# A two-block hybrid network on one core: the first three products in plain fp32, running totals on VectorE, decay triangles by a product, and a port rule in the planner

## The chip, the cores and the metric

The kernel runs on one core of a Trainium2 chip. The metric is the device time in microseconds (us) of one execution, the median of several. The engines are TensorE (PE; PEld is its weight load), VectorE (DVE), ScalarE (ACT), GpSimd (POOL), and SyncE (SP), which here only issues DMAs. In fp32r a 32-bit operand takes one pass through TensorE; a plain fp32 operand takes a slower form, which the profile records as two matmul records for each product.

## The reference, cut to what matters

Two blocks of two layers each run over 272 tokens (16 meta tokens and 256 of the sequence, width 1024), later over 256. The first layer is a gated delta rule, and its start is what the change touches:

```
a_in = rms_norm(hs, norm_w[0, 0])
proj = a_in @ w_in                      # q, k, v, z, and 2 x 16 gate columns
g = -exp(a_log) * softplus(proj[gates] + dt_bias)
G = cumsum(g)                           # in chunks
decay = exp(where(i >= j, G_i - G_j, -inf))
a_mat = I + (k_i . k_j) beta_i * decay * strict ;  attn = (q_i . k_j) * decay
```

After it come an output product, an RMS norm, the residual, a convolutional FFN of width 2816, an mLSTM layer and a second such FFN. The second block has short convolution and windowed attention, a SwiGLU FFN, gated linear attention with latent attention, and another SwiGLU FFN; each of its four parts ends in a LayerNorm.

## The kernel before

Activations lie transposed: 128 features on the partitions, tokens along the free axis, eight tiles of 128 for width 1024. The weights stream from HBM in 413 chunks of 512 KB, and one chunk is eight tiles of 128x128, which is one output tile of a product over 1024 features. Every chunk (`wload`, from L309) is split in two fp32r halves: ACT copies the raw tile to `wh` (L325), DVE subtracts to get `wl` (L326). An activation is split likewise into `xh` and `xl`. A product is then three fp32r matmuls (`mm3`): wh with xh, wh with xl, wl with xh. There are three raw buffers, and a raw buffer is free once both halves are made.

**The opening** (`first_raw`, then `pre_norm` called from `gdn`). x times the norm's weight is split without waiting for the row statistic, and three products start from it: the 32 gate columns and two tiles of q and k. `group` interleaves them (L372 to L375); the results are multiplied by 1/rms afterwards (L525). In the same time DVE and ACT write the normed x and its split (L479, L473, L474), from which all further products run. From the gates come the decays: for each of four groups of heads DVE makes `gl` (three instructions, L712), PE sums it along the tokens with plain fp32 products (L716), ACT takes the exponential (called on L717, recorded as L270) and POOL multiplies by a triangle of ones (L718), twelve times in all.

**The norms.** `post_norm` runs the output product tile by tile; ACT squares, and POOL adds the squares into a running total `acc` (`acc_sq`, L444). After the last tile a column sum of `acc` and one of the last square go to one PSUM bank, DVE forms mean + eps (`rse` L552, `rsv` L553), POOL raises to the power -1/2 (L554), PE broadcasts (L429). Then, for each of the eight tiles, DVE multiplies (`xn` L561) and adds the residual (`hs` L563), ACT makes `xh` (L567), DVE `xl` (L568), ACT the next square (L571), and POOL adds it to the next running total; meanwhile PE runs the next layer's first products from `xh` and `xl` through `group`. Three of the four calls have this second total. `warm` puts dummy products on PE meanwhile (L414). `layer_norm` has its running totals on POOL too (L1251, L1259, L1265), eleven additions in each of four calls.

**The order of the work.** `IssueOrder` takes all instructions, gives each a modelled cost, and simulates the five engines forward and backward, three rounds; `fix` then ties each engine's instructions in the order found. That fixes the order within each engine. Between engines only data and buffers order the work, at run time. In its model VectorE and GpSimd share a port: an instruction in `port` waits while the other engine's one is running.

Of the kernel before, what the change touches and what calls it, by code (L numbers as in the profile page):

```python
# [6 lines left out]
F32 = mybir.dt.float32  # L7
F32R = mybir.dt.float32r
AF = mybir.ActivationFunctionType
ALU = mybir.AluOpType  # L10
# [248 lines left out]
class Kern:  # L259
# [49 lines left out]
    def wload(self, first, need, ahead):  # L309
# [3 lines left out]
        while self.wloaded <= need or (self.wloaded <= need + ahead and self.wloaded < self.io["w"].shape[0]):  # L313
# [13 lines left out]
            self.wchunks[self.wloaded] = (h, l)  # L327
            self.wloaded += 1

    def wnext(self, first=None):  # L330
        ci, j = divmod(self.wpos, CH)
        self.wpos += 1
        if j == 0:
            self.wload(ci if first is None else first, ci, self.ahead if first is None else 0)
        h, l = self.wchunks[ci]
        return h[:, j], l[:, j]
# [104 lines left out]
    def acc_sq(self, acc, prev, sq, m):  # L441

        if m and m < KD - 1:
            self.nc.gpsimd.tensor_tensor(acc, prev if m == 1 else acc, sq, ALU.add)  # L444

    def rsqrt(self, v, pool):
        V = self.nc.vector
# [34 lines left out]
    def first_raw(self, pool):  # L482

        nc, n = self.nc, T1
        raw = [pool.tile([128, 4, T1], F32R, name="xr", tag="of", bufs=4) for _ in range(4)]
        xh, xl = [lambda k, a=a: raw[a + k // 4][:, k % 4] for a in (0, 2)]
        sqs = [pool.tile([128, 2, 2, T1], F32, name="kq", bufs=4) for _ in range(2)]
        st = self.pst.tile([128, 512], F32, name="st")[:, :n]
        for k in range(KD):
            hs = self.hs[:, k]  # L490
            nc.scalar.activation(xh(k), hs, AF.Copy, scale=self.p("nw00", k))
            nc.vector.scalar_tensor_tensor(xl(k), hs, self.p("nw00", k), xh(k).bitcast(F32), ALU.mult, ALU.subtract)
            if k % 2:
                j = k // 2
                sq, hs = [a.rearrange("p a b t -> p (a b) t")[:, 2 * (j % 2):2 * (j % 2) + 2] for a in (sqs[j // 2],)][0], self.hs[:, k - 1:k + 1]
                if j % 2:
                    nc.vector.tensor_tensor(sq, hs, hs, ALU.mult)
                else:
                    nc.scalar.activation(sq, hs, AF.Square)
                if j:  # L500
                    nc.vector.tensor_tensor(acc, acc, sq, ALU.add)
                else:
                    acc = sq
        for i in range(2):
            self.stat_add(st, acc[:, i], i == 0, i == 1)
        return st, lambda k: (xh(k), xl(k))

    def pre_norm(self, wname, t0, pool, items, outs, dest=None, st=None, tag="rsy"):

        nc, n = self.nc, T1 - t0  # L510
        s = [] if st is None else [st]

        def hook():
            if not s:
                s.append(self.row_stat(*self.nacc, n))

        raw = self.group(items, hook)
        r = self.rstd(s[0], n, D, pool, tag)
        xh, xl = dest or [pool.tile([128, KD, n], F32R, name=a) for a in ("xnh", "xnl")]
        outs = list(outs(raw))  # L520
        for k in range(KD):
            self.scaled(k, xh, xl, wname, t0, n, r, pool)
            if k and outs:
                o, ps, p, t = outs.pop(0)
                nc.vector.tensor_tensor(o, ps, r[:p, t:], ALU.mult)  # L525
        assert not outs
        return lambda k: (xh[:, k, :n], xl[:, k, :n])

    def post_norm(self, wname, K, x, t0, pool, nxt, tag='mix'):

        nc, n = self.nc, T1 - t0
        V = nc.vector
        mixt = [pool.tile([128, 4, T1], F32, name="mix", tag=tag + (str(i + 1) if tag == "PT" else ""), bufs=1 if tag == "PT" else 2)
                for i in range(2)]
        mix = lambda m: mixt[m // 4][:, m % 4, :n]
        acc = self.small.tile([128, T1], F32, name="acc")[:, :n]
        prev = None
        first = self.halves(x, n) if K == 16 else []
        for m in range(KD):
            ps = first.pop(0) if first else self.proj(K, x, n)  # L540
            sq = pool.tile([128, T1], F32, name="sq", bufs=2)[:, :n]
            nc.scalar.activation(sq, ps, AF.Square)
            nc.scalar.activation(mix(m), ps, AF.Copy, scale=self.p(wname, m))
            self.acc_sq(acc, prev, sq, m)
            prev = sq
        self.lnexp()
        c = len(starts(n))
        st = self.bank()
        self.stat_cols(st, acc, n)
        self.warm(6, self.stat_cols(st[:, c:], sq, n))  # L550
        e, v = [self.small.tile([128, 4], F32, name=a)[:, :c] for a in ("rse", "rsv")]
        V.tensor_scalar(e, st[:, 0:c], 1.0 / D, 1e-6, ALU.mult, ALU.add)  # L552
        V.scalar_tensor_tensor(v, st[:, c:2 * c], 1.0 / D, e, ALU.mult, ALU.add)  # L553
        nc.gpsimd.tensor_tensor(v, v, self.c("nhalf")[:, :c], ALU.pow)  # L554
        r = self.pst.tile([128, 512], F32, name="st")[:, :n]
        self.warm(8, self.bcast(r, v, n))
        xh, xl = self.xsplit()
        acc = self.small.tile([128, T1], F32, name="acc")[:, :n]
        for m in range(KD):
            t = pool.tile([128, T1], F32, name="xn", bufs=2)[:, :n]  # L560
            V.tensor_tensor(t, mix(m), r, ALU.mult)  # L561
            hs = self.hs[:, m, t0:]
            V.tensor_tensor(hs, hs, t, ALU.add)  # L563
            if nxt is None:
                self.split(xh[:, m, :n], xl[:, m, :n], hs)
                continue
            nc.scalar.activation(xh[:, m, :n], hs, AF.Copy, scale=self.p(nxt, m))  # L567
            V.scalar_tensor_tensor(xl[:, m, :n], hs, self.p(nxt, m), xh[:, m, :n].bitcast(F32), ALU.mult, ALU.subtract)  # L568
            sq = (self.small.tile([128, T1], F32, name="sql", bufs=1) if m == KD - 1 else
                  pool.tile([128, T1], F32, name="sq", bufs=2))[:, :n]  # L570
            nc.scalar.activation(sq, hs, AF.Square)  # L571
            self.acc_sq(acc, prev, sq, m)
            prev = sq
        self.nacc = (acc, sq)
        return lambda k: (xh[:, k, :n], xl[:, k, :n])
# [41 lines left out]
    def gdn(self):  # L617
# [5 lines left out]
        with ExitStack() as es:  # L623
# [11 lines left out]
            for t in Ufs + X64s:  # L635
# [6 lines left out]
            ba = v_first[0:32, 2]  # L642
            wg = pool.tile([128, KD, 32], F32, name="wg", tag="o1")
            nc.scalar.dma_start(wg, self.io["wg"].rearrange("p (k m) -> p k m", m=32))
            wgs = pool.tile([128, 2, KD, 32], F32R, name="wgs", tag="vs1")
            wgh, wgl = wgs[:, 0], wgs[:, 1]
            self.split(wgh, wgl, wg)
            x = self.pre_norm("nw00", 0, pool, [(xr, T1, 32, True, [(wgh[:, k], wgl[:, k]) for k in range(KD)]), (xr, T1, 128, False), (xr, T1, 128, False)],
                              lambda ps: [(ba, ps[0], 32, 0), (v_first[:, 0], ps[1], 128, 0), (v_first[:, 1], ps[2], 128, 0)],
                              self.xsplit(), st, "cv")  # L650
            ba16 = pool.tile([32, 4, 32], F32, name="cv", bufs=2)
            G.memset(ba16, 0.0)
            V.tensor_copy(ba16[:, :, 0:16], ba[:, 0:16].unsqueeze(1).to_broadcast([32, 4, 16]))
# [49 lines left out]
            strict = pool.tile([128, 2, 128], F32, name="strict", tag="o0")  # L703
            V.tensor_tensor(strict[:, 0], self.ones, self.c("tri"), sub)
            V.tensor_tensor(strict[:, 1], self.c("blk16"), self.c("tri16"), sub)
            for g in range(4):
                eg_ = pool.tile([128, 9, 128], F32, name=f"E{g}")
                gl = pool.tile([128, 9, 128], F32, name="gl_", tag=("PT0", "PT1", "PT2", "vs0")[g])
                for c in range(3):
# [2 lines left out]
                    V.tensor_tensor(gl[:, u], strict[:, c // 2].unsqueeze(1).to_broadcast([128, nn, 128]),  # L712
                                    gg[:, 9 * g + 4 * c:9 * g + 4 * c + nn].unsqueeze(2).to_broadcast([128, nn, 128]), mult)
                    tp = bank().rearrange("p (h i) -> p h i", h=4)
                    for h in range(nn):
                        TE.matmul(tp[:, h], gl[:, 4 * c + h], self.c("tri" if c < 2 else "tri16"), start=True, stop=True)  # L716
                    self.act(eg_[:, u], tp[:, 0:nn], AF.Exp)  # L717
                    G.tensor_tensor(eg_[:, u], eg_[:, u], self.c("tri" if c < 2 else "tri16").unsqueeze(1).to_broadcast([128, nn, 128]), mult)  # L718
                E.append(eg_)

            self.silu()
# [496 lines left out]
    def layer_norm(self, name, K, x, pool, last=False, tags=("xr0", "xr1", "xr2", "xr3")):  # L1218
# [27 lines left out]
        def square(m):  # L1246
# [1 line left out]
            sq = tmp("lnsq", 3)  # L1248
            nc.scalar.activation(sq, X[:, m], AF.Square)
            if 1 <= m < KD - 1:  # L1250
                GP.tensor_tensor(ac2, prev if m == 1 else ac2, sq, add)  # L1251
            prev = sq

        for m in range(KD):
            ps = self.proj(K, x, n)
            if m < 4:
                V.scalar_tensor_tensor(X[:, m], X[:, m], ALPHA, ps, mult, add)
                if m:
                    GP.tensor_tensor(ac, X[:, 0] if m == 1 else ac, X[:, m], add)  # L1259
            else:  # L1260
                V.tensor_tensor(X[:, m], X[:, m], ps, add)
                square(m)
                not_normed(m)
                if 4 < m < KD - 1:
                    GP.tensor_tensor(ac, X[:, 4] if m == 5 else ac, X[:, m], add)  # L1265
            if m == 3:
                st = self.pst.tile([128, 512], F32, name="st")[:, :n]
                self.stat_add(st, ac, True, True)
# [432 lines left out]
class IssueOrder:  # L1701
# [207 lines left out]
    def forward(self, due, look=0):  # L1909
# [30 lines left out]
        while True:  # L1940
# [13 lines left out]
            if best > 100.0:  # L1954
                wait[e].remove(chosen)
                heapq.heapify(wait[e])
                push(now[e], chosen[1:])
            d, k = pop(now[e])
            t = max(t, ready[k])
            if self.port[k] and owner != e:  # L1960
                t = max(t, shared)
# [110 lines left out]
```

## Time and profile before

| what | value |
|---|---|
| median of 3 runs | 1469.59 us (1467.21 to 1471.34) |
| the profiled execution | 1478.24 us, of which 1476.40 us from first to last instruction |
| PE, DVE, ACT, POOL busy | 98%, 71%, 57%, 13% |
| mean granted clock of TensorE | 0.988 of full speed |
| weights moved | 413 chunks, 220.34 MB read, 150 GB/s over the span |

Busy shares are of the span. PE's records overlap, since matmuls are pipelined: one 272-column fp32r matmul lasts 0.29 us in the records while the next starts 0.125 us behind it. A granted clock of 1.00 is 2.4 GHz, 0.50 is 1.2 GHz. A line number is a line of the kernel before.

### The profile page before, as it was taken

What the parts mean: (1) busy time and instruction counts of PE and PEld (TensorE: products, weight loads), DVE (VectorE), ACT (ScalarE), POOL (GpSimd) and SP (SyncE); (2) the same over time, 40 slices, a digit from 0 to 9 for tenths busy, and PEclk for the clock granted to TensorE, in tenths of its full rate; (3) what the DMA queues carried; (4) which work ended last, traced back from release to release, by engine and by line L of the source; (5) the groups of instructions that cost most, each with busy time, mean ns of one, the idle gap of its engine ahead of it and who ended that gap; (6) DMA issues with size and microseconds to landing.
All of it is one profiled execution on the core that took longest, in us unless ns stands there. A gap on an engine that the chain in (4) does not pass through costs nothing.

```text
span 1476.4 us, 30582 instructions
## 1 busy us (share of the span) xinstructions
PE 1442.6 (98%) x12258; PEld 1397.4 (95%) x12258; DVE 1053.9 (71%) x1972; ACT 841.9 (57%) x1568; POOL 189.7 (13%) x286
## 2 busy tenths in 40 slices
PE   8999999999999999999999999999999999999997
PEld 7888999998999999899999998999999978999997
DVE  8987486549998358567998456686556798975553
ACT  5546467556766446556776446565454566654442
POOL 1563004121000120003000000020002100300011
PEclk9989999999999999999999999999999999999999
DMA  4333334244655543423565553447555324375551
GB/s 164 120 104 119 101 93 131 87 156 155 211 188 165 179 143 129 144 86 129 192 201 189 190 158 115 159 133 228 188 184 183 130 84 157 121 235 189 185 187 57
DMA packets 72669, 223.95 MB, mean 152 GB/s; under 512 B 16784, under 2 KB 18896, under 8 KB 72400
## 3 DMA queue, kind: packets, MB, share of 16 engines
q1 hardware_dynamic: 71952, 220.38, 45.9%
q8 instruction: 96, 1.57, 0.4%
q10 hardware_dynamic: 576, 1.62, 0.3%
q14 instruction: 45, 0.37, 0.1%
HBM read 220.34 MB, written 1.64 MB: 150 GB/s over the span
## 4 chain that ended last, share of the span: by engine, by line
PE 86%; DVE 8%; DMA 2%; ACT 1%; POOL 1%; issue 1%; SPq 0%; ACTq 0%; DVEq 0%; POOLq 0%
PE acc L349 18%; PE acc L350 18%; PE acc L351 18%; PE psa L349 3%; PE psa L350 3%; PE psa L351 3%; PE psb L351 2%; PE psb L350 2%; PE psb L349 2%; DVE wl L326 2%; PE acc L375 2%; PE acc L372 1%; PE acc L373 1%; DMA wraw<-in_w_dram 1%; DVE kq L726 1%
## 5 line engine op out<-in xcount | busy, mean ns | idle before, releaser
L326 DVE TENSOR_TENSOR wl<-wraw,wh 128x1024 fp32r<-128x1024 f32 x413 | 508.4, 1233 | 231.5 <-ACT wh L325 230.6
L325 ACT ACTIVATE wh<-wraw 128x1024 fp32r<-128x1024 f32 x413 | 435.2, 1056 | 309.6 <-PE acc L350 176.8
L349 PE MATMUL acc<-xh,wh 128*128 128x256 f32 (+1 forms) x848 | 246.4, 291 | 2.1 <-DVE kq L726 2.1
L351 PE MATMUL acc<-xh,wl 128*128 128x256 f32 (+1 forms) x848 | 246.7, 291 | 1.7 <-DVE wl L326 1.7
L350 PE MATMUL acc<-xl,wh 128*128 128x256 f32 (+1 forms) x848 | 246.3, 291 | 0.1
L350 PE MATMUL acc<-al,wh 128*128 128x256 f32 (+1 forms) x704 | 197.3, 282 | 0.0
L349 PE MATMUL acc<-ah,wh 128*128 128x256 f32 (+1 forms) x704 | 197.2, 282 | 0.0
L351 PE MATMUL acc<-ah,wl 128*128 128x256 f32 (+1 forms) x704 | 196.6, 283 | 0.0
L349 PEld LDWEIGHTS acc<-xh,wh 128*128 128x128 f32 x848 | 161.4, 190 | 5.1 <-issue 1.9
L351 PEld LDWEIGHTS acc<-xh,wl 128*128 128x128 f32 x848 | 161.6, 191 | 3.7 <-DVE wl L326 2.1
L350 PEld LDWEIGHTS acc<-xl,wh 128*128 128x128 f32 x848 | 161.1, 190 | 1.9 <-issue 1.0
L349 PEld LDWEIGHTS acc<-ah,wh 128*128 128x128 f32 x704 | 132.4, 189 | 0.1
L350 PEld LDWEIGHTS acc<-al,wh 128*128 128x128 f32 x704 | 132.3, 189 | 0.0
L351 PEld LDWEIGHTS acc<-ah,wl 128*128 128x128 f32 x704 | 131.8, 188 | 0.1
L349 PE MATMUL acc<-xnh,wh 128*128 128x272 f32 (+1 forms) x424 | 122.2, 288 | 0.0
L350 PE MATMUL acc<-xnl,wh 128*128 128x272 f32 (+1 forms) x424 | 122.1, 288 | 0.0
L351 PE MATMUL acc<-xnh,wl 128*128 128x272 f32 (+1 forms) x424 | 121.7, 287 | 0.0
L349 PE MATMUL acc<-oh,wh 128*128 128x256 f32 (+2 forms) x304 | 86.7, 291 | 1.5 <-ACT oh L473 1.5
L350 PE MATMUL acc<-ol,wh 128*128 128x256 f32 (+2 forms) x304 | 87.1, 289 | 0.0
L351 PE MATMUL acc<-oh,wl 128*128 128x256 f32 (+2 forms) x304 | 87.0, 289 | 0.0
L349 PEld LDWEIGHTS acc<-xnh,wh 128*128 128x128 f32 x424 | 79.8, 188 | 1.2 <-issue 1.0
L350 PEld LDWEIGHTS acc<-xnl,wh 128*128 128x128 f32 x424 | 80.0, 189 | 0.9 <-issue 0.7
(700 smaller groups left out, 3456.8 us busy)
## 6 DMA issues: line engine op xcount, KB each, us to landing
wraw<-in_w_dram SPq DMA_DIRECT2D x413, 512.0 KB, 3.5
late<-in_late_dram ACTq DMA_DIRECT2D x1, 1205.5 KB
hs<-in_x_dram SPq DMA_DIRECT2D x4, 272.0 KB
out_dram<-hs SPq DMA_DIRECT2D x8, 128.0 KB, 1.9
d<-PT SPq DMA_DIRECT2D x32, 9.0 KB, 1.6
cst<-in_cst_dram SPq DMA_DIRECT2D x1, 339.5 KB
A<-d SPq DMA_DIRECT2D x4, 72.0 KB
d<-Xb SPq DMA_DIRECT2D x4, 72.0 KB
```

What stands on the lines that cost most here:

```text
L325: nc.scalar.activation(h, raw, AF.Copy)
L326: nc.vector.tensor_tensor(l, raw, h.bitcast(F32), ALU.subtract)
L349: mm(ps, h, xh, start=start, stop=False)
L350: mm(ps, h, xl, start=False, stop=False)
L351: mm(ps, l, xh, start=False, stop=stop)
L372: mm(o, h, x(k)[0], start=k == 0, stop=False)
L373: mm(o, l, x(k)[0], start=False, stop=False)
L375: mm(o, w[k][0][:, :m], x(k)[1], start=False, stop=k == KD - 1)
L726: V.scalar_tensor_tensor(out[:, d:], ps[:, :T1 - d], cw(3 - d), out[:, d:], mult, add)
```

## The change

Five edits. (1) The gate product and the first two q and k tiles take the raw weights and the unsplit x, in plain fp32: 24 matmuls in place of 72; no split of x times norm weight, of the gate weights, or of the first two chunks, which stay in their raw buffers until their last product. (2) The running totals of the norms move from POOL to DVE. (3) In `post_norm` the two column sums go to two banks, and `rse` stands between them. (4) A product of the identity with a matrix of 0 and -2^100 opens each decay bank, so the exponential gives the triangle, and POOL's twelve multiplications go. (5) The planner's forward pass may hold a DVE instruction that uses the port, when a GpSimd port instruction with an earlier due time becomes ready within its length.

```diff
+    def wplain(self):
+        assert self.wpos == self.wloaded * CH
+        raw = self.wp.tile([128, CH, 128], F32, name="wraw", bufs=3)
+        self.nc.sync.dma_start(raw, self.io["w"][self.wloaded])
+        self.wloaded += 1
+        self.wpos += CH
+        return raw
...
-            self.nc.gpsimd.tensor_tensor(acc, prev if m == 1 else acc, sq, ALU.add)
+            self.nc.vector.tensor_tensor(acc, prev if m == 1 else acc, sq, ALU.add)
...
-            nc.scalar.activation(xh(k), hs, AF.Copy, scale=self.p("nw00", k))
-            nc.vector.scalar_tensor_tensor(xl(k), hs, self.p("nw00", k), xh(k).bitcast(F32), ALU.mult, ALU.subtract)
+            nc.scalar.activation(xr(k), hs, AF.Copy, scale=self.p("nw00", k))
...
-        st = self.bank()
+        st, s2 = self.bank(), self.bank()
+        e, v = [self.small.tile([128, 4], F32, name=a)[:, :c] for a in ("rse", "rsv")]
         self.stat_cols(st, acc, n)
-        self.warm(6, self.stat_cols(st[:, c:], sq, n))
-        e, v = [self.small.tile([128, 4], F32, name=a)[:, :c] for a in ("rse", "rsv")]
         V.tensor_scalar(e, st[:, 0:c], 1.0 / D, 1e-6, ALU.mult, ALU.add)
-        V.scalar_tensor_tensor(v, st[:, c:2 * c], 1.0 / D, e, ALU.mult, ALU.add)
+        self.warm(6, self.stat_cols(s2, sq, n))
+        V.scalar_tensor_tensor(v, s2[:, 0:c], 1.0 / D, e, ALU.mult, ALU.add)
...
+            ws = [wg] + [self.wplain() for _ in range(2)]
+            ps = [self.bank()[:32, :T1]] + [self.pacc.tile([128, 512], F32, name="acc")[:, :T1] for _ in range(2)]
+            for k in range(KD):
+                for o, w in zip(ps, ws):
+                    TE.matmul(o, w[:, k], xr(k), start=k == 0, stop=k == KD - 1)
...
+            far = pool.tile([128, 3, 128], F32R, name="far")
+            for i, a in enumerate(("tri", "tri16")):
+                V.tensor_scalar(far[:, i], self.c(a), 2.0 ** 100, -2.0 ** 100, mult, add)
+            V.tensor_copy(far[:, 2], ident)
...
+                    TE.matmul(tp[:, 0:nn], far[:, 2], far[:, c // 2].unsqueeze(1).to_broadcast([128, nn, 128]), start=True, stop=False)
                     for h in range(nn):
-                        TE.matmul(tp[:, h], gl[:, 4 * c + h], self.c("tri" if c < 2 else "tri16"), start=True, stop=True)
+                        TE.matmul(tp[:, h], gl[:, 4 * c + h], self.c("tri" if c < 2 else "tri16"), start=False, stop=h == nn - 1)
                     self.act(eg_[:, u], tp[:, 0:nn], AF.Exp)
-                    G.tensor_tensor(eg_[:, u], eg_[:, u], self.c("tri" if c < 2 else "tri16").unsqueeze(1).to_broadcast([128, nn, 128]), mult)
...
-                GP.tensor_tensor(ac2, prev if m == 1 else ac2, sq, add)
+                V.tensor_tensor(ac2, prev if m == 1 else ac2, sq, add)
...
             d, k = pop(now[e])
+            if look and e == DVE and self.port[k]:
+                rival = min(((dq, max(r, free[POOL]), q) for r, dq, q in wait[POOL] + [(ready[q], dq, q) for dq, q in now[POOL]]
+                             if self.port[q]), default=None)
+                if rival is not None and rival[0] < d and rival[1] < t + self.time[k] and rival[1] > t:
+                    other = min(((dq, q) for dq, q in now[e] if not self.port[q] and t + self.time[q] < rival[1] + 200), default=None)
+                    wait_end = rival[1] + self.time[rival[2]]
+                    gain = max(wait_end - rival[0] + t + self.time[k] - rival[1], t + self.time[k] - d) - \
+                        max(wait_end - rival[0], wait_end + self.time[k] - d)
+                    if gain > 100.0:
+                        push(now[e], (d, k))
+                        if other is None:
+                            free[e] = max(rival[1] + 1, t + 1)
+                            continue
+                        now[e].remove(other)
+                        heapq.heapify(now[e])
+                        d, k = other
```

The two other totals of `layer_norm` (L1259, L1265) move in the same way.

## Rows read from the trace of the kernel before

**Rows 1.** The page, part 1: each engine's busy time and share of the span.
```profile
PE 1442.6 (98%) x12258; PEld 1397.4 (95%) x12258; DVE 1053.9 (71%) x1972; ACT 841.9 (57%) x1568; POOL 189.7 (13%) x286
```

**Rows 2.** Stages: stretch, length, busy (instructions) of PE, PEld, DVE, ACT, POOL, clock, DMA.
```profile
7.40:11.30 3.90, 1.89 (x7) 0.97 (x6) 3.65 (x8) 3.15 (x6) 0.00 (x0) 1.00 0.97 380
11.30:14.40 3.10, 2.74 (x11) 2.13 (x12) 3.03 (x6) 2.59 (x6) 1.44 (x2) 0.51 0.07 26
22.00:91.90 69.90, 64.55 (x608) 60.79 (x606) 68.92 (x190) 37.74 (x71) 36.33 (x64) 1.00 0.36 113
91.90:106.50 14.60, 12.44 (x137) 11.56 (x137) 8.89 (x23) 5.57 (x13) 7.62 (x25) 0.55 0.23 57
352.00:1464.40 1112.40, 1104.07 (x8939) 1078.52 (x8937) 794.89 (x1381) 638.66 (x1115) 82.37 (x83) 1.00 0.50 163
```

**Rows 3.** Waits of PE: total us, times, longest.
```profile
PE st L429 <- POOL rsv L554: 2.9, 3, 1.0
PE psa L375 <- DVE xl L568: 1.9, 2, 1.6
PE acc L375 <- DVE xl L568: 1.7, 2, 1.3
```

**Rows 4.** Timeline of the opening: start, us, engine, line.
```profile
8.08 0.31 PE L372 MATMUL psb<-xr,wgs 128*32 128x272 f32 x1 [0.64 <-ACT wgs L473]
22.03 0.29 PE L349 MATMUL acc<-xh,wh 128*128 128x272 f32 x1
9.01 2.59 DVE L492 SCALAR_TENSOR_TENSOR xr<-hs,fst,xr 128x272 fp32r<-128x272 f32 x6
13.65 5.25 SPq L317 DMA_DIRECT2D wraw<-in_w_dram  x3
```

**Rows 5.** The chain of waits after the first output product: start, us.
```profile
331.72 0.17 DVE rse L552
332.16 1.79 POOL rsv L554
346.66 0.46 PE st L405 x2
```

**Rows 6.** Timeline of two 512-column products at the full clock.
```profile
1231.39 0.40 PE L1588 MATMUL acc<-wh,xh 128*128 128x512 f32 x1
1231.62 0.40 PE L1589 MATMUL acc<-wl,xh 128*128 128x512 f32 x1
```

**Rows 7.** DVE groups while POOL masks, 37 to 57.5 us: busy, mean ns.
```profile
L326 DVE TENSOR_TENSOR wl<-wraw,wh 128x1024 fp32r<-128x1024 f32 x5 | 7.9, 1587 | 0.0
L712 DVE TENSOR_TENSOR gl__451<-strict,gg 128x512 f32<-128x512 f32 x2 | 2.6, 1345 | 0.0
L712 DVE TENSOR_TENSOR gl__428<-strict,gg 128x128 f32<-128x128 f32 x1 | 1.0, 954 | 0.0
```

**Rows 8.** By line over the whole run: ns min/median/max.
```profile
L326 DVE TENSOR_TENSOR wl<-wraw,wh x413: 1183/1224/1909, 12.4 to 1448.4; 128x1024 fp32r<-128x1024 f32 x138
L712 DVE TENSOR_TENSOR gl__405<-strict,gg x3: 274/678/680, 34.3 to 36.3; 128x512 f32<-128x512 f32 x2, 128x128 f32<-128x128 f32 x1
L444 POOL TENSOR_TENSOR acc<-acc,sq x35: 741/835/1635, 305.0 to 868.3; 128x272 f32<-128x272 f32 x20, 128x258 f32<-128x258 f32 x10, 128x256 f32<-128x256 f32 x5
L554 POOL TENSOR_TENSOR rsv<-rsv,fst x4: 703/1820/1924, 332.2 to 876.6; 128x3 f32<-128x3 f32 x3, 128x2 f32<-128x2 f32 x1
L563 DVE TENSOR_TENSOR hs<-hs,xn x32: 416/432/1012, 335.6 to 885.4; 128x272 f32<-128x272 f32 x16, 128x258 f32<-128x258 f32 x8, 128x256 f32<-128x256 f32 x8
```

**Rows 9.** Busy time (as Rows 2) in the residual pass, first and last of three.
```profile
334.80:346.70 11.90, 9.98 (x69) 8.87 (x69) 11.69 (x24) 7.41 (x17) 5.00 (x6) 1.00 0.14 48
681.90:692.80 10.90, 10.45 (x84) 10.16 (x84) 10.80 (x24) 6.39 (x16) 5.21 (x6) 1.00 0.13 47
```

**Rows 10.** Busy time (as Rows 2) in the first LayerNorm.
```profile
955.00:990.00 35.00, 35.00 (x297) 34.95 (x296) 31.41 (x63) 23.32 (x52) 12.27 (x12) 1.00 0.33 108
```

**Rows 11.** DMA issues of the first 16 us, median us to landing.
```profile
wraw<-in_w_dram SPq DMA_DIRECT2D x5, 512.0 KB, 7.1
```

More of the change, by code (lines that the diff above doesn't have):

```diff
@@ L484, in first_raw @@
         nc, n = self.nc, T1
-        raw = [pool.tile([128, 4, T1], F32R, name="xr", tag="of", bufs=4) for _ in range(4)]
-        xh, xl = [lambda k, a=a: raw[a + k // 4][:, k % 4] for a in (0, 2)]
+        raw = [pool.tile([128, 4, T1], F32, name="xr", tag="of", bufs=4) for _ in range(2)]
+        xr = lambda k: raw[k // 4][:, k % 4]
         sqs = [pool.tile([128, 2, 2, T1], F32, name="kq", bufs=4) for _ in range(2)]
@@ L505, in first_raw, with pre_norm @@
             self.stat_add(st, acc[:, i], i == 0, i == 1)
-        return st, lambda k: (xh(k), xl(k))
-    def pre_norm(self, wname, t0, pool, items, outs, dest=None, st=None, tag="rsy"):
+        return st, xr
+    def pre_norm(self, wname, t0, pool, items, outs, dest=None, st=None, tag="rsy", raw=None):
         nc, n = self.nc, T1 - t0
@@ L515, in hook @@
                 s.append(self.row_stat(*self.nacc, n))
-        raw = self.group(items, hook)
+        raw = self.group(items, hook) if raw is None else raw
         r = self.rstd(s[0], n, D, pool, tag)
@@ L644, in gdn @@
             nc.scalar.dma_start(wg, self.io["wg"].rearrange("p (k m) -> p k m", m=32))
[L645 to L648, printed above, removed]
+            ws = [wg] + [self.wplain() for _ in range(2)]
[3 more added lines that the diff above has]
+                    TE.matmul(o, w[:, k], xr(k), start=k == 0, stop=k == KD - 1)
+            x = self.pre_norm("nw00", 0, pool, None,
                               lambda ps: [(ba, ps[0], 32, 0), (v_first[:, 0], ps[1], 128, 0), (v_first[:, 1], ps[2], 128, 0)],
-                              self.xsplit(), st, "cv")
+                              self.xsplit(), st, "cv", ps)
             ba16 = pool.tile([32, 4, 32], F32, name="cv", bufs=2)
@@ L1258, in layer_norm @@
                 if m:
-                    GP.tensor_tensor(ac, X[:, 0] if m == 1 else ac, X[:, m], add)
+                    V.tensor_tensor(ac, X[:, 0] if m == 1 else ac, X[:, m], add)
             else:
@@ L1264, in layer_norm @@
                 if 4 < m < KD - 1:
-                    GP.tensor_tensor(ac, X[:, 4] if m == 5 else ac, X[:, m], add)
+                    V.tensor_tensor(ac, X[:, 4] if m == 5 else ac, X[:, m], add)
             if m == 3:
```

## The prediction

> **What bounds the kernel now.** I read the page's busy shares first: TensorE is busy 98% of the span [rows 1]. So an engine beside it counts only where PE stands still or runs at the low clock. The busy time by stage finds those places [rows 2]. From 352 to 1464 us PE idles 8.3 of 1112.4 us. From 22.0 to 91.9 us it idles 69.9 - 64.55 = 5.35 us while DVE is busy 68.92 us: there DVE is the bound, not PE. From 7.4 to 11.3 us PE works 1.89 of 3.9 us, and from 11.3 to 14.4 us its granted clock is 0.51, nearly all at 1.2 GHz, behind that gap. From 91.9 to 106.5 us it is 0.55. The list of PE's waits shows the third place [rows 3]: 1.9 + 1.7 = 3.6 us for `xl` in the residual pass of `post_norm`, and 2.9 us for the power on POOL. The change touches these places.
>
> **The change part by part**, made against the profiled execution: 1476.40 us of span and 1.84 us around it, 1478.24 us, which is 8.65 us above the median of the runs, 1469.59 us. I carry the saving over to the median unchanged.
>
> *The first products.* Before, the first of the 72 fp32r matmuls starts at 8.08 us and the first product of the normed x at 22.03 us [rows 4]. A plain fp32 product of 272 columns holds PE 0.46 us (the pair of records in the chain, [rows 5]); 24 of them take 11.0 us, and the statistic's two, which fall in the same stretch, 0.9 us. No ACT or DVE split stands before them: wg was there before 8.08 us, since its split had to precede that matmul. From 8.1 us they end at 20.1 us at full clock: **-1.9 us** against 22.03. The bounds: at 1.2 GHz all through they end 12 us later; with an earlier start 0.5 us sooner.
>
> The page "FP8 and Floating Point Precision" of the Trainium skill, "TensorE Precision Notes", gives true fp32 four passes. An fp32r product of 512 columns starts 0.23 us after the one before [rows 6], so 272 columns and four passes would be an estimated 0.49 us, and by that page this term would be -1.2 us. The measured pair is used.
>
> *The triangles.* Twelve identity products join the decays: eight of 512 columns at 0.23 us [rows 6] and four of 128, which I put at 0.1 us (between a quarter of 0.23 and the 0.12 that 272 columns would take). 1.84 + 0.4 = **+2.2 us** of PE, between 0 if all of it falls into PE's idle time and 2.4 us. They need constants alone, so nothing waits for them.
>
> *DVE in the opening.* Eight `xl` go (six take 2.59 us, so 0.43 each, 3.4 us [rows 4]); two `wl` splits at 1.2 us (2.4 us) and the gate weights' split (about 0.4 us, it has 256 columns). POOL's masking goes, and with it the time that DVE lost beside it: between 37 and 57.5 us five `wl` splits averaged 1587 ns, two 512-wide `gl` 1345 ns and a 128-wide one 954 ns [rows 7], against 1224, 678 and 274 ns elsewhere [rows 8]: 5 x 0.36 + 2 x 0.67 + 0.68 = 3.8 us. `far` costs three short instructions of at most 0.27 us, 0.8 us. Together DVE is relieved of 3.4 + 2.4 + 0.4 + 3.8 - 0.8 = 9.2 us before 92 us. PE had 5.35 us of idle time there to win. The relief exceeds it, but the chain from the statistic through the gates to the decays stays on DVE, so I take 60%: **-3.2 us**, between 0 (PE's waits only move) and -5.35.
>
> *The residual pass.* For each tile DVE owes `xn`, `hs` and `xl`, and it is busy 11.69 of 11.9 us in the first pass and 10.80 of 10.9 in the last [rows 9]; 24 instructions at the unhindered 0.43 us of a 272-column `hs` [rows 8], or less where they overlap, make 10.3 at most, so at least 1.4 us of the first pass is waiting for POOL's six totals of 0.84 us [rows 8]. They now cost DVE six times up to 0.43 us, 2.6 us. DVE's total hardly falls. What changes is what can wait: before, a POOL addition stopped whichever `xl` stood beside it; now the addition is an instruction of DVE's own order, and the `xl` that PE wants can go first, since the total is wanted only near the end of PE's 15 us of first products. PE's 3.6 us of waiting for `xl` [rows 3] should mostly go; I take three quarters, **-2.7 us**, between 0 (the additions go ahead of the splits) and -3.6.
>
> *The separate bank.* `rse` (0.17 us, [rows 5]) leaves the chain between the last column sum and the power, in four calls: **-0.7 us**. If the order puts something else there, 0.
>
> *The port rule.* The power takes 1.79 us in that chain [rows 5] and 1.82 at the median, against 0.70 in the fourth call, which has two columns instead of three and no split beside it [rows 8]: a `wl` split, issued right after `rsv`, holds the port. The rule holds such a split in the simulation; `fix` then records only that the split follows `rsv` and comes before `xn`, which is so already. On the chip DVE, having nothing to wait for, would issue it at the same moment. I take **0**. If it did work, three calls would win 1.1 us each, -3.3 us; the other end is that instructions it moves cost as much, +3.3.
>
> The page "SBUF — State Buffer" of the Trainium skill, "SBUF: two separate sides", says that whichever of the two starts first has the shared port pair for the whole instruction and the other blocks fully. The rows agree on the size of the wait, and by that rule this term is 0, where the planner's own model would have -3.3 us. That is the third rival.
>
> *The LayerNorms.* Eleven additions a call move to DVE, which is busy 31.41 of 35 us in the first, while PE is busy 35.00 of 35.00 [rows 10]. At 0.43 us they add 4.7 us at most, and 11 POOL instructions that DVE waited beside go. PE's stock of products covers it: **0**, with up to 0.5 us a call lost if the cover runs out, 2 us in all.
>
> *The new order.* The planner searches again, so every instruction can move. What it can touch elsewhere is PE's 8.3 us of idle time after 352 us and the low-clock stretch from 91.9 to 106.5 us, where (1 - 0.55) x 14.6 = 6.6 us go to the clock [rows 2]. I put **0**, with 4 us either way.
>
> The sum: -1.9 + 2.2 - 3.2 - 2.7 - 0.7 = -6.3 us: 1471.9 us by the profile, **1463.3 us** as a median.
>
> **The rivals.**
>
> 1. *Small gains, no visible change.* DVE's additions go ahead of the `xl` splits and PE's waits in the opening only move: -1.9 + 2.2 - 1.6 - 0.7 = -2.0, 1467.6 us. For it: DVE has no slack in the residual pass. Against: PE's waits for `xl` come in few long pieces (1.6 and 1.3 us, [rows 3]), as a badly placed instruction gives them.
>
> 2. *Slower: the raw buffers are held.* Before, the next weight loads are issued at 13.65 us, when the first split has freed a raw buffer [rows 4]. Now two of the three raw buffers stay until their products end. If the products are interleaved by k, both come free only near 20.1 us; a load in the opening took 7.1 us to land [rows 11], then come a split of 1.2 us on DVE [rows 8] and one on ACT before it, say 1.1: 29.5 us. PE has one chunk in stock, three matmuls of 0.12 us for each of eight tiles, to 23.0 us. It would stand 6.5 us, and a stand has been followed by the low clock: another 6.6 us as from 91.9 us [rows 2]. -6.3 + 13.1 = +6.8, 1476.4 us. Against it: the planner knows the buffers and can finish one chunk's eight products first, by some 13 us, and a load outside the crowded start should land sooner. It decides from the point where the fourth chunk is split later than 23 us.
>
> 3. *The port rule works, or the low clock after 91.9 us goes.* The power drops to 0.7 us: -9.6, 1460.0 us. Without the low-clock stretch 6.6 us more than the forecast: 1456.7 us; both, 1453.4. For it: relieved DVE and POOL shift that stretch's work. Against: nothing in the change is aimed at the latter, and the order is fixed within engines only.
>
> **How the numbers follow.** What this kernel's runs can tell from no change is about 0.3%, 4.4 us: faster means below 1465.2 us, slower above 1474.0. The forecast has 0.52, with a range of its own from 1459 to 1467.5, of which 0.05 lies within 0.3%; rival 1 has 0.22, all within; rival 2 0.11, slower; rival 3 0.15, faster. Faster 0.47 + 0.15 = 0.62, same 0.27, slower 0.11. The range from 1453.5 to 1472 leaves out rival 2 and the far end of rival 3.
>
> **What would show each step.** The first product of the normed x at 20 us and no granted clock near 0.5 before it; above 22 the first step is wrong. PE's idle time from there to the same work as before 91.9 us falls from 5.35 to about 2 us. `gl` takes 0.68 us for 512 columns throughout. PE's waits for `xl` (L568) fall from 3.6 us to about 1. The power stays near 1.8 us in three calls; at 0.7 the port rule did what I deny. The LayerNorms show no PE idle. The forecast fails if the fourth chunk's split comes after 23 us, or if a new low-clock stretch appears.

## The result and the profile after

The changed kernel takes 1462.11 us (median of 7 runs, 1458.90 to 1466.11), the kernel before beside it 1471.34 (7 runs, 1467.21 to 1476.79): ratio 0.994, 95% interval 0.9924 to 0.9955. Forecast: 1463.3. The sign and the size were right. The places were right for half of it: in the two profiled executions the first power comes 16.7 us sooner, and the stretch behind it, where the forecast had gains as well, is 3.5 us longer.

The page of the changed kernel, part 1 (answers to [rows 1]); POOL lost more than half of its work, DVE gained 4 us:

```profile
PE 1437.6 (98%) x12246; PEld 1391.4 (95%) x12246; DVE 1058.0 (72%) x2050; ACT 838.8 (57%) x1565; POOL 86.2 (6%) x188
```

Stages of the changed kernel (columns as in [rows 2]). The first: the opening with the fp32 products. The second: to the inverse's first product, which before stood at 89.0 us. The third to fifth answer to the last row of [rows 2], [rows 10] and the first of [rows 9]. The last two split the span at the first power:

```profile
8.00:20.48 12.48, 12.48 (x52) 7.71 (x50) 9.55 (x24) 5.39 (x12) 0.79 (x2) 1.00 0.41 151
20.48:82.50 62.02, 60.51 (x466) 58.14 (x464) 58.27 (x164) 35.07 (x66) 17.50 (x42) 1.00 0.43 127
335.30:1451.30 1116.00, 1106.60 (x8938) 1080.90 (x8936) 806.78 (x1454) 637.08 (x1114) 7.98 (x9) 0.99 0.50 163
942.20:977.20 35.00, 35.00 (x297) 34.95 (x297) 32.74 (x75) 23.56 (x52) 0.87 (x1) 1.00 0.37 121
318.10:330.00 11.90, 9.81 (x73) 9.19 (x73) 11.18 (x31) 8.11 (x19) 0.00 (x0) 1.00 0.09 34
0.00:315.49 315.49, 310.39 (x3158) 291.29 (x3159) 227.19 (x536) 184.48 (x419) 75.72 (x177) 1.00 0.40 125
315.49:1463.10 1147.61, 1127.18 (x9090) 1100.08 (x9088) 830.86 (x1515) 654.34 (x1147) 10.44 (x11) 0.99 0.49 161
```

The same split of the kernel before:

```profile
0.00:332.16 332.16, 317.82 (x3172) 299.89 (x3173) 234.58 (x538) 187.20 (x422) 99.84 (x196) 0.96 0.38 119
332.16:1476.30 1144.14, 1124.76 (x9088) 1097.46 (x9086) 819.31 (x1435) 654.73 (x1146) 89.84 (x91) 1.00 0.49 161
```

Take length less PE's busy time. Up to the first power PE's idle time falls from 14.3 to 5.1 us; behind it it is 19.4 before and 20.4 after. The rest of the 16.7 us by which the first power comes earlier is 7.4 us of PE's busy time, and that is clock (0.96 before, 1.00 after), less the work that the change adds to PE there. Behind the power PE's busy time is 2.4 us up for the same products, and that is clock too, above all one stretch behind a stand that none of the other traces has (a wait and a stretch of the changed kernel):

```profile
PE psa L1146 <- ACT ex L270: 1.7, 1, 1.7
589.50:600.00 10.50, 10.50 (x39) 7.94 (x40) 5.45 (x18) 3.95 (x17) 0.00 (x0) 0.55 0.27 94
```

PE's waits in the changed kernel (total us, times, longest; answers to [rows 3]):

```profile
PE psa L381 <- ACT xnh L482: 2.5, 1, 2.5
PE acc L384 <- DVE xl L576: 1.4, 1, 1.4
PE st L438 <- POOL rsv L562: 0.7, 1, 0.7
PE psa L384 <- DVE xl L576: 0.3, 1, 0.3
```

Waiting for `xl` fell from 3.6 to 1.7 us, for the power from 2.9 to 0.7. The first row, a stand of 2.5 us at 341 us, is new. By line, over the whole run (ns min/median/max; answers to [rows 8]):

```profile
L728 DVE TENSOR_TENSOR gl__345<-strict,gg x3: 283/683/684, 31.3 to 33.7; 128x512 f32<-128x512 f32 x2, 128x128 f32<-128x128 f32 x1
L562 POOL TENSOR_TENSOR rsv<-rsv,fst x4: 696/850/1771, 315.5 to 864.0; 128x3 f32<-128x3 f32 x3, 128x2 f32<-128x2 f32 x1
L571 DVE TENSOR_TENSOR hs<-hs,xn x32: 416/428/442, 318.9 to 872.9; 128x272 f32<-128x272 f32 x16, 128x258 f32<-128x258 f32 x8, 128x256 f32<-128x256 f32 x8
```

`gl` and `hs` have lost their long ends: no 512-wide `gl` of the four groups (one is shown) takes over 0.69 us, where [rows 7] has 1.35, and no `hs` over 442 ns (1012 before). DVE no longer waits beside POOL there. The power is short in two of the three long calls.

### The profile page after: what moved, and what is told of

It is laid out like the page before. It is cut to its first block, busy times and chain, and to the rows that moved or that the text cites. A ratio compares the mean times of both kernels' runs of the same rounds, so it can differ in the third digit from the quotient of the medians.

```text
span 1463.2 us, 30475 instructions
## 1 busy us (share of the span) xinstructions
PE 1437.6 (98%) x12246; PEld 1391.4 (95%) x12246; DVE 1058.0 (72%) x2050; ACT 838.8 (57%) x1565; POOL 86.2 (6%) x188
## 4 chain that ended last, share of the span: by engine, by line
PE 89%; DVE 6%; DMA 2%; ACT 1%; POOL 1%; issue 1%; SPq 0%; DVEq 0%; ACTq 0%; POOLq 0%
PE acc L358 18%; PE acc L359 18%; PE acc L360 18%; PE psa L358 3%; PE psa L360 3%; PE psa L359 3%; PE psb L358 3%; PE psb L360 3%; PE psb L359 3%; DVE wl L326 1%; PE acc L384 1%; PE acc L381 1%; PE acc L382 1%; DMA wraw<-in_w_dram 1%; PE acc L423 1%
## 5 line engine op out<-in xcount | busy, mean ns | idle before, releaser
L326 DVE TENSOR_TENSOR wl<-wraw,wh 128x1024 fp32r<-128x1024 f32 x411 | 501.3, 1222 | 214.1 <-ACT wh L325 212.2
```

The source lines that it names most:

```text
L326: nc.vector.tensor_tensor(l, raw, h.bitcast(F32), ALU.subtract)
```

## The experiments

Every kernel ran beside the kernel before. e1 to e4 ran on one chip, e5 to e8 on a second, e9 to e12 on a third. "PE idle" is length less busy time in the one profiled execution of each, up to the first power and behind it (± 0.1). "Clock loss" is span x (1 - granted clock), the mean over the kernel's runs; the three chips gave 8.8 to 9.5 us for the kernel before (81 runs). A fit over 202 runs, with a constant for each kernel on each chip, gives 0.69 ± 0.04 us of span per us of clock loss; "at full clock" is that constant, ± 0.5 to 0.8 us.

| kernel | ratio (95%) | PE idle, to / behind the first power | clock loss | at full clock |
|---|---|---|---|---|
| before | 1 | 14.3 / 19.4 | 8.8 to 9.5 | 1461.6 to 1462.6 |
| changed | 0.994 (0.9924 to 0.9955) | 5.1 / 20.4 | 7.3 | 1455.4 |
| e1, without the port rule | 0.9937 (0.9923 to 0.9951) | 4.9 / 20.5 | 6.1 | 1454.2 |
| e2, port rule alone | 1.0015 (0.9997 to 1.0032) | 10.7 / 20.9 | 7.8 | 1464.9 |
| e3, without fp32 products | 0.9941 (0.9923 to 0.9959) | 6.7 / 18.7 | 4.6 | 1455.9 |
| e4, fp32 products alone | 0.9997 (0.9984 to 1.0011) | 11.3 / 18.8 | 8.4 | 1461.2 |
| e5, before again | one run | 13.9 / 18.6 | 13.2 | |
| e6, triangles alone | 1.0025 (1.0010 to 1.0041) | 9.8 / 20.6 | 12.9 | 1463.4 |
| e7, totals alone | 0.9998 (0.9986 to 1.0010) | 14.5 / 20.7 | 8.9 | 1463.1 |
| e8, triangles and totals | 0.9997 (0.9987 to 1.0007) | 9.4 / 20.8 | 10.9 | 1461.4 |
| e9, separate bank alone | 0.9990 (0.9976 to 1.0004) | 13.2 / 18.4 | 7.3 | 1461.9 |
| e10, without separate bank | 0.9969 (0.9953 to 0.9984) | 3.7 / 20.9 | 8.9 | 1458.4 |
| e11, before, one round more | 0.9994 (0.9979 to 1.0010) | 11.4 / 19.0 | 8.8 | 1462.7 |
| e12, changed, one round more | 0.9958 (0.9942 to 0.9974) | 6.3 / 20.7 | 7.1 | 1457.8 |

**e1 and e2: the port rule.** In e1 the rule is taken out of the changed kernel; in e2 it alone is put into the kernel before.

```diff
-            if look and e == DVE and self.port[k]:
-                rival = min(...)
...
```

> The changed kernel with the planner's port rule taken out; the rest of the change stays. Changed kernel: 1462.1 us, powers of 1.77, 0.85, 0.85 and 0.70 us. The prediction's theory: the rule does nothing on the chip, and the two short powers come from the new order alone, so the powers stay 0.85 us in the second and third call and the time is 1462 (1460 to 1464). Rival: the rule made them short; then both are back at 1.8 to 1.9 us, PE waits 1.0 us longer at each, and the time is 2.0 us up, 1464.

> The kernel before with the port rule alone. The prediction's theory: no effect, powers 1.8 to 1.9 us in three calls, 1471 us as before (ratio 1.000). Rival: the rule works, the power is 0.85 us in two or three calls, 2 to 3 us less, 1468 to 1469 (ratio 0.998). Up to 90 us the order on PE is that of the kernel before, so this also shows whether the stand of 2.2 us at 91.9 us and the 13 us at half clock after it belong to that order (they come again within a few us) or to that one execution (they are gone).

Without the rule the powers are again 1.77, 0.85, 0.85 and 0.70 us, and the time is the same; alone it gives no gain (1.0015). The prediction's 0 for the rule stands and the rival falls. e2 had a third power of 0.85 us, which looked like the rule, until e5 showed it in the kernel before.

**e3 and e4: the plain fp32 products.** e3 is the changed kernel with the split x, the split gate weights and 72 fp32r matmuls; e4 puts only the fp32 products into the kernel before.

```diff
-            ws = [wg] + [self.wplain() for _ in range(2)]
...
+            self.split(wgh, wgl, wg)
+            x = self.pre_norm("nw00", 0, pool, [(xr, T1, 32, True, ...
```

> The changed kernel with the first three products as before: split x, split gate weights, 72 fp32r matmuls, two more weight splits. The prediction's theory: the first normed product is back at 22 us, with a clock near 0.5 at 11 to 14 us (1.9 us lost), and of DVE's relief before 92 us 6.2 of 9.2 us go, two thirds of 3.2 us, 2.1 us more: 4.0 us up, 1466.1. Rival: what is won before 22 us is only part of a stock that a later wait uses up, so at most 1.5 us stay: 1462 to 1463.6.

> The kernel before with the first three products in plain fp32 alone. The prediction's theory: first normed product at 20.1 to 20.5 us, no clock near 0.5 before it, 4.0 us down from 1471.3: 1467.3 (ratio 0.997). Rival 1: only the first 1.5 to 1.9 us stay, 1469.6. Rival 2: with DVE earlier the stand at 91.9 us and the low clock behind it go as well, 6.6 us more: 1460.7 (ratio 0.993).

Neither moved the time, so the prediction's 4 us for this part fall, and rival 2 of e4 too. The expectation of e3 failed in its event as well: the first normed product was to be back at 22 us with a low clock before it, and it starts sooner than in the changed kernel (20.48), at the full clock. Start, us, and the stretch before it:

```profile
19.00 0.29 PE L349 MATMUL acc<-xh,wh 128*128 128x272 f32 x1
0.00:19.00 19.00, 17.66 (x117) 16.51 (x118) 14.53 (x29) 10.70 (x20) 5.99 (x15) 1.00 0.70 244
```

So an early first normed product doesn't need the plain fp32 products: e6 and e8, which lack them too, have it at 18.88 and 18.66 us. Why nothing is left in e4 can be read from its own waits and its DVE groups between 20 and 60 us (busy, mean ns):

```profile
PE acc L360 <- DVE wl L326: 3.2, 3, 1.7
PE psb L727 <- DVE gl__341 L723: 1.2, 1, 1.2
PE psa L727 <- DVE gl__341 L723: 1.0, 1, 1.0
```

```profile
L326 DVE TENSOR_TENSOR wl<-wraw,wh 128x1024 fp32r<-128x1024 f32 x6 | 9.0, 1507 | 0.0
L723 DVE TENSOR_TENSOR gl__341<-strict,gg 128x512 f32<-128x512 f32 x2 | 3.5, 1756 | 0.0
```

PE reaches the decays sooner and stands there 2.2 us for `gl`, which takes 1.76 us beside POOL's masks instead of 0.68. What was won early is waited off at DVE: up to the first normed product and from there to the inverse's first product PE idles 3.4 + 5.3 us in before and 1.05 + 7.7 in e4, which is the same sum.

```profile
0.00:20.60 20.60, 19.55 (x92) 14.63 (x93) 12.07 (x25) 10.77 (x22) 4.95 (x15) 1.00 0.59 209
20.60:90.16 69.56, 61.83 (x459) 58.21 (x457) 66.43 (x165) 34.87 (x66) 33.78 (x56) 0.98 0.36 115
```

With the masks gone (e1 against e3) the products are worth 1.8 us of PE's idle time before the first power, 4.9 against 6.7; the total times don't tell those two apart.

**e5: the kernel before once more**, no edit.

> The kernel before, unchanged, profiled a second time. If the stand of 2.2 us at 91.9 us and the 13.7 us at half clock after it come from the order of the instructions, they come again within a microsecond or two; if they belong to that one execution, they are gone, and the span is near 1468 instead of 1476.4 us. The run with the port rule alone, whose order is the same on PE to 90 us, showed neither, so the second is expected.

The first was true, against my expectation. The stand is there again, in the middle of 72 small products of the inverse, with a low clock behind it. Waits and a stretch of e5:

```profile
PE psa L887 <- issue: 1.8, 1, 1.8
85.00:110.00 25.00, 23.16 (x369) 21.49 (x370) 19.46 (x54) 12.47 (x28) 15.86 (x49) 0.86 0.41 110
```

e11 ran the same products without a break:

```profile
85.00:110.00 25.00, 25.00 (x410) 23.65 (x409) 23.24 (x59) 17.00 (x38) 18.89 (x52) 1.00 0.51 143
```

The stand showed in before, e5, e6, e7 and e8 (0.9 to 2.8 us), not in e2, e9, e11 or the changed kernel. It comes again at the same product in before and e5, but the order doesn't decide it: in e2, e9 and e11 PE runs the same order as in before from the start to beyond these products, and they have no stand. What does separate the traces is where they ran: all four of the second chip have it, none of the eight of the other two. The chip of before's first profile isn't on record, and no other kernel has a second trace, so the cause stays open. Its low clock varies from run to run: 13.7 us at half clock in the first profile of before, 6.8 in e5.

**e6, e7 and e8: triangles and totals**, each alone in the kernel before, then both.

```diff
-                    G.tensor_tensor(eg_[:, u], eg_[:, u], ...tri..., mult)
+                    TE.matmul(tp[:, 0:nn], far[:, 2], far[:, c // 2]..., start=True, stop=False)
...
-            self.nc.gpsimd.tensor_tensor(acc, prev if m == 1 else acc, sq, ALU.add)
+            self.nc.vector.tensor_tensor(acc, prev if m == 1 else acc, sq, ALU.add)
```

> The kernel before with the decay triangles by a product alone. The prediction's terms: +2.2 us for PE's twelve products and -0.6 x 3.0 us for what DVE no longer loses beside POOL, +0.4: 1469 (ratio 1.000). Rival: the masks on POOL carry the gain, since DVE is the bound from 22 to 92 us: gl takes 0.68 us throughout, PE's idle time there falls from 5.3 to under 2 us and the time by 4 to 6 us, 1463 to 1465 (ratio 0.997 to 0.996).

> The kernel before with the running totals on VectorE alone (post_norm and LayerNorm). The prediction's term: PE's 3.6 us of waits for xl in the residual pass fall to about 1, -2.7 us: 1466 (ratio 0.998), LayerNorms unchanged. Rival 1: the additions cost DVE as much as they free, no change, 1468.6. Rival 2: DVE gains in all places where POOL's totals stood beside it, the LayerNorms too, 5 us or more, 1463 (ratio 0.9965).

> The kernel before with the triangles and the totals, without the plain fp32 products, the separate bank and the port rule. Since the fp32 products alone gave 0.9997 and the port rule alone 1.0015, these two should carry nearly the whole gain of the change: ratio 0.994 to 0.995, 1460 to 1461. Rival: the gain needs all parts together (an order that only all of them allow); then it stays at 0.997 or above, 1464 or more.

In e6 every 512-wide `gl` takes at most 0.69 us, PE's waits for DVE's convolution (`kq`, 2.1 us in e5) are gone, and its idle time up to the first power is 9.8 us against 10.7 to 14.5 in the traces with neither triangles nor fp32 products. The DVE relief is real. From the first normed product to the inverse's first PE idles 2.9 us:

```profile
18.88:83.17 64.29, 61.36 (x461) 58.45 (x459) 60.53 (x174) 36.34 (x70) 15.03 (x40) 0.97 0.38 112
```

The time is up all the same: PE has twelve products more, and the clock loss is the largest of all, 12.9 us, which at 0.69 is 2.5 us over that of before. e7 brought what its term named, waits for `xl` down from 3.6 to 1.9 us, and no time: PE stands 1.7 us at 355 us, where before has no stand. e8's expectation failed plainly: two parts that are in every fast kernel give nothing by themselves.

**e9 and e10: the separate bank**, alone in the kernel before, and taken from the changed kernel.

```diff
-        st = self.bank()
+        st, s2 = self.bank(), self.bank()
```

> The kernel before with the separate bank for the second column sum alone. So far the runs that have the bank beside triangles and totals (without the fp32 products 0.9941, without the port rule 0.9937) are 0.6% down, and triangles with totals but without the bank 0.9997. Theory A: the bank itself carries the gain, 0.995 to 0.996, 1464. Theory B, the prediction's term: -0.7 us, ratio 0.9995, and the gain comes only where triangles, totals and bank meet.

> The changed kernel with both column sums in one bank as before, the rest of the change kept. Theory A, that the bank carries the gain: 0.999, 1469 to 1470. Theory B (-0.7 us for the bank): 0.9945, the changed kernel's 0.994 less 0.0005. A value between, 0.997, would say that the order that the planner finds for each set of edits is worth as much as the edits.

Theory A falls: alone it is 0.9990. That e10 came out between is the case named last in its expectation. But the bank does one thing that can be read directly. In e10 the first three powers take 1.77, 1.79 and 1.78 us; in e9 1.77, 0.86 and 0.85. The second power of e9 (start, us):

```profile
533.00 0.16 DVE L553 SCALAR_TENSOR_TENSOR rsv<-psb,rse 128x3 f32<-128x3 f32 x1 [0.72 <-PE psb L421]
533.24 0.86 POOL L554 TENSOR_TENSOR rsv<-rsv,fst 128x3 f32<-128x3 f32 x1 [7.88 <-DVE rsv L553]
533.37 1.23 DVE L326 TENSOR_TENSOR wl<-wraw,wh 128x1024 fp32r<-128x1024 f32 x1 [0.21 <-ACT wh L325]
```

and the second of e10, the same place:

```profile
528.02 0.16 DVE L561 SCALAR_TENSOR_TENSOR rsv<-psb,rse 128x3 f32<-128x3 f32 x1
528.19 1.22 DVE L326 TENSOR_TENSOR wl<-wraw,wh 128x1024 fp32r<-128x1024 f32 x1
528.33 1.79 POOL L562 TENSOR_TENSOR rsv<-rsv,fst 128x3 f32<-128x3 f32 x1 [212.10 <-DVE rsv L561]
```

DVE's order is the same in both. With `rse` out of the chain the power starts while ACT is still making the split's input `wh`, so POOL comes 0.13 us first; else DVE comes 0.14 us first. The second power is 0.85 or 0.86 us in all five traces with the bank (changed, e1, e3, e9, e12) and 1.79 to 1.94 in the nine without; the third goes both ways on either side (1.84 in e3, with the bank). It is a race of tenths of a microsecond, and the kernel before decides it differently from run to run: third power 1.92 us in its first profile, 0.85 in e5:

```profile
675.51 0.16 DVE L553 SCALAR_TENSOR_TENSOR rsv<-psa,rse 128x3 f32<-128x3 f32 x1
675.75 0.85 POOL L554 TENSOR_TENSOR rsv<-rsv,fst 128x3 f32<-128x3 f32 x1 [2.37 <-DVE rsv L553]
676.00 1.23 DVE L326 TENSOR_TENSOR wl<-wraw,wh 128x1024 fp32r<-128x1024 f32 x1 [0.33 <-ACT wh L325]
```

**e11 and e12: the same instructions in another order.**

```diff
-        o.fix(o.search(10, 3)[1])
+        o.fix(o.search(10, 4)[1])
```

> The kernel before with four of the planner's rounds in place of three: the same instructions in another order. It gauges what a new order alone is worth. Theory A, orders matter little: within 0.1% of before, 1469 to 1472. Theory B, an order is worth up to 3 us either way (the port rule alone, which changes nothing but the order, gave 1.0015): 0.998 or 1.002, with the stand at 92 us or the gaps near 290 us changed.

> The changed kernel with four rounds in place of three: the same gauge on the other side. Theory A: ratio 0.994 again. Theory B: 0.992 to 0.996. If it comes near 0.998, a good part of the gain of the change is its order and not its edits.

e11 shows no change of time, though the stand is gone and PE's idle time before the first power is 11.4 instead of 13.9 us in e5. e12 loses 0.18% of the changed kernel's 0.6%, about 2.6 us; its interval and the changed kernel's overlap, and e2's 0.15% is no clearer of nothing. At full clock the two are 2.4 and 3.3 us. So an order alone can be worth some 2.5 us here, close to the largest single terms of the forecast; both of these were losses, and no run shows a gain by an order alone. The parts alone (e2, e4, e6, e7, e9) add up to +0.25%, the whole change gives -0.6%. So the gain is not a sum of parts; PE's idle time before the first power names the common place: 9.4 us or more wherever a part stands alone or the bank and fp32 products are both missing (e8, 1.5 us of it the stand above), 6.7 or less in the changed kernel and its variants.

## Why the prediction was right

The sum of -6.3 us against -8.8 measured (0.6% of 1470): at full clock the change is worth 6.8 us (1455.4 against a mean of 1462.2), and 1.9 us less clock loss give 1.3 more, 8.1 together. The profiled execution of before had a clock loss of 17.4 us against a mean of 9.2: at 0.69 that is 5.7 of the 8.65 us by which it lay above the median, and part of why the two profiles differ by 13.2 us. That the total came so near is luck in part: the opening gave more than its terms, the residual pass next to nothing, and no term held the 1.3 us of clock. Step by step:

- **First products, -1.9.** First normed product at 20.48 us, 20.1 forecast, at full clock throughout. Right in time, wrong in its cause and as a gain: e3 reaches that product sooner without the plain fp32 form (19.00 us), and the runs give the form nothing alone and nothing that can be told when it is left out.
- **Triangles +2.2, DVE relief -3.2.** PE's idle time to the inverse's first product was to fall to about 2 us; it is 62.02 - 60.51 = 1.5. The mechanism was right: from the first normed product to the inverse's first PE idles 4.8 to 5.7 us in the six traces with neither triangles nor fp32 products, 2.9 to 3.4 with the triangles and not the fp32 products (e3, e6, e8), 7.7 the other way round (e4), and 1.3 to 2.5 with both (changed, e1, e10, e12). So the relief is the triangles'; the fp32 products add to it only where the masks are gone. Up to the first power idle time falls by 9.2 us against the first profile of before, 5.6 to 8.9 against its other orders and e5, but not all of that is relief. 2.2 us are the stand at 92 us, and 2.1 us come off PE's waits near 290 us before the output product (`oh` and `o`, 2.6 us in before, 0.5 in the changed kernel), at which no edit aimed: e2, with another order alone, has them at 0.5 as well. In turn before, the changed kernel and e2 (total us, times, longest):

```profile
PE acc L349 <- ACT oh L473: 1.5, 1, 1.5
PE psb L1067 <- DVE o L1066: 1.1, 1, 1.1
PE psb L1083 <- DVE o L1082: 0.5, 2, 0.3
PE psb L1067 <- DVE o L1066: 0.5, 1, 0.5
```

- **Residual pass, -2.7.** The step that failed. The waits for `xl` did fall, from 3.6 to 1.7 us, but not in the first pass (1.4 us, 1.3 before), where PE idles 2.1 us instead of 1.9; and 26 us behind the first power PE stands 2.5 us. The chain there in the changed kernel (start, us, what), and ACT's wait between 330 and 350 us:

```profile
334.16 8.10 DMA wraw<-in_w_dram
...
342.28 1.06 ACT wh L325
343.33 0.33 ACT xnh L482
```

```profile
ACT wh L325 <- DMA wraw<-in_w_dram: 5.5, 2, 4.4
```

ACT, first in line for the next products' input `xnh`, waits 4.4 us for a weight chunk. From ACT's queue the two FFN parameter transfers (176 and 1205 KB) are issued 16.1 and 19.5 us behind the power; in before 12.9 and 16.6. In the seven traces with totals (changed, e1, e3, e7, e8, e10, e12) it is 16.1 to 16.2, and each has a stand of 1.5 to 2.5 us about 26 us behind the power; the six without totals and with 12.4 to 12.9 have none, and e6, at 16.3, has two of 0.7 and 0.9. The packets in the trace show how: in the changed kernel that chunk is on its way from 20.3 to 25.5 us behind the power, beside the larger transfer (21.1 to 26.6); in before it takes from 21.6 to 23.2, when that transfer is ending (18.6 to 23.0). ACT's order does the rest: before has six `xnh` ahead of this chunk's `wh` and comes to it at 26.2 us, 3 us after the chunk has landed; the changed kernel has three and waits. Moving the transfers or the `wh` alone wasn't tried. I had looked only at PE's waits inside the pass, not at what ACT issues behind it.
- **Separate bank, -0.7.** PE's wait for the powers is 1.9 us in e5 and 0.7 in e9. Right in direction, by a mechanism that I hadn't seen (the race), and larger in PE's waits; in time e9 alone (0.9990) isn't clear of nothing.
- **Port rule, 0.** Right in time (e1, e2). The reason was half right: DVE does issue the split as soon as it can, but where `wh` comes later than `rsv`, that is when `wh` is there and not at once.
- **LayerNorms, 0.** PE busy 35.00 of 35.00 again, DVE 32.74. Right.
- **New order, 0 with 4 either way.** The bounds held (e2, e11, e12); how much of the change's own gain is its order isn't shown.
- **Rival 2, raw buffers held.** Its condition was met: the fourth chunk's split came at 24.81 us, past the 23 us that I had named. It cost 0.45 us, not 6.5. PE filled the time with the three identity products of the first decay group (23.86 to 24.6 us), which need constants alone, and with the two products of each trio that don't want `wl`:

```profile
23.86 0.40 PE L731 MATMUL psa<-far 128*128 128x512 f32 x1
24.81 1.22 DVE L326 TENSOR_TENSOR wl<-wraw,wh 128x1024 fp32r<-128x1024 f32 x1
26.08 0.40 PE L360 MATMUL acc<-xh,wl 128*128 128x272 f32 x1 [0.45 <-DVE wl L326]
```

What stays open: why e10 is 0.3% behind the changed kernel with less idle time in its profile (its waits for the powers are 2.9 us against 0.7, which would be 2.2 of the 3.0 us at full clock), and how much of the 6.8 us belongs to each part. No run leaves only the triangles, or only the totals, out of the changed kernel, so whether the totals help it at all isn't shown. Orders are worth up to some 2.5 us and the intervals are ±0.15%, so runs of this kind can't divide it.

## What to carry to other kernels

Where an order is searched anew, gauge first what a new order of the same instructions is worth, and don't credit a part with less. Where two engines limit a stage in turn, relieving one can be worth nothing until the other is relieved too (e4), so test the parts together as well as alone, and leave each out of the whole once. After a wait has gone, look for the next stand at all queues of the engines moved, DMA issues among them, not only in the stage itself.

## What the runs showed of the hardware

The granted clock accounts for 60% of the variance between runs of one kernel (the fit above). The clock loss differs between kernels, from 4.6 us in e3 to 12.9 in e6, and doesn't simply follow PE's idle time: e10 has the least of it before the first power and loses 8.9.

The port was not held for the whole of the power. In e5 it starts at 675.75 and lasts 0.85 us; DVE's split starts 0.25 us into it and takes its usual 1.23 us. The other way round the power does wait: 1.92 us at 679.12 beside a split from 679.11 to 680.34. The Trainium skill, "SBUF — State Buffer", "SBUF: two separate sides", has the one that starts first keep the shared ports for its whole instruction while the other blocks. The trace agrees where DVE is first, and not where this small POOL instruction is, as far as the recorded ends of POOL's instructions can be trusted.
